# A decoder layer in fp32: an input tile issued earlier, two output tiles moved into the attention, and the last MLP group taken by token tile

## The chip, the cores and the metric

One core of a Trainium2 chip runs the whole layer. The metric is the device time of one execution in microseconds (us). The engines are TensorE (PE, with its weight loads as PEld), VectorE (DVE), ScalarE (ACT), GpSimd (POOL) and SyncE (SP), which here issues every DMA. Each engine runs its own list of instructions in a fixed order and waits on semaphores of the others.

## The reference

```python
c_act = jax.nn.silu(c)
mod = c_act @ w_mod[l] + b_mod[l]                     # 2048 x 12288
sh1, sc1, g1, sh2, sc2, g2 = split(mod, 6)
h = rmsnorm(x, attn_norm_g) * (1.0 + sc1) + sh1       # x: 256 x 2048
proj = h @ w_in                                       # 2048 x 1856
o_a = swa_sink_attention(q_a, k_a, v_a, sinks, rel_bias)   # 16 heads of 64, window 128
c_q, c_kv = rmsnorm(cq part), rmsnorm(ckv part)       # ranks 384 and 128
q_b, kv_b = c_q @ w_uq, c_kv @ w_ukv
o_b = mla_attention(...)                              # 8 heads, causal
x = x + g1 * (concat(o_a, o_b) @ w_out)               # 2048 x 2048
h = rmsnorm(x, mlp_norm_g) * (1.0 + sc2) + sh2
x = x + g2 * (relu(h @ w_ff1) ** 2 @ w_ff2)           # 2048 x 8192 x 2048
return rmsnorm(x, final_norm_g)
```

All of it is float32; a sequence has 256 tokens.

## The kernel before

The 256 tokens lie along the free axis, and the 2048 features are 16 tiles of 128 partitions (`kt`). Every weight is read once, in tiles of about 1 MB, through two rings of buffers: `wm` (tag `rawm`, two slots, and four more in stage 1) for w_mod, and `raw` (three slots) for the rest. All DMAs are issued by SP in program order; one that needs a slot holds up those behind it. The program is written in one order; a scheduler then sets the order of the rows on each engine, and that order is fixed at run time.

*Modulation.* The product with w_mod is not on TensorE: VectorE multiplies a 128 x 2048 tile with the broadcast conditioning vector and sums it (L168, `mod_col`), which gives 128 values of one of the six modulation vectors. 96 such tiles are strewn over the program. Part 1 and 0 (for h) come in stage 1, part 2 (g1) in the attention, parts 4 and 3 (for the second h) in the out projection, part 5 (g2) in the MLP; g2 then goes through DRAM (`g_dr`, a scatter of single elements) to be read back as a row.

*Stage 1.* Step kt takes two modulation tiles, forms h (xn on VectorE L256, h on ScalarE L258), and multiplies it with one w_in tile `wi` in 30 matmul records (L269). The program issues the modulation tiles of kt + 1 ahead of the `wi` tile of kt.

*Attention.* Units 0 to 7 are sliding-window heads (scores L407, minima L336 on VectorE, exponentials on ScalarE, a scaling of the rows L357 on ScalarE or VectorE in turn, transposition L377, values L422), units 8 to 11 the latent heads (`scb`, `ssb`, `ptb`, `pob`). Between them stand fillers, the up-projections from cq and ckv (`pvb`, `puqr`, `pukn`, `puqn`), which need the norms `rq` and `rkv` (`rmsn`, whose last step is L323). Each unit leaves its output in `mix`, split in two parts (L387, L388); mix 0 holds the sliding heads, mix 1 the latent ones.

*Out projection.* Matmuls that need full precision run in a faster form on two-part operands. `split` writes the high part of half a weight tile on ScalarE (L192) and the rest on VectorE (L193). Half 0 takes mix 0, half 1 mix 1; each has 16 output tiles of 24 matmuls (L198 to L200) and an addition to the residual `x_sb` on VectorE (L656). Then the second norm (`r_a`, `r_y`: L180 to L183, with Ln and Exp on ScalarE) lets the MLP's h begin (xn L678 or on GpSimd L680 and L681, h L682 on ScalarE and its second part L683 on VectorE).

*MLP.* ff1's first quarter runs over kt (`pf`), the rest by output tile (`pu`, L204 and L205), ff2 in four q by four column groups c (`pd`, L785 to L787), each group with two PSUM banks, one for each tile t of 128 tokens. In the last group (q = 3, c = 3) VectorE multiplies by g2 (L799), adds the residual (L800) and multiplies by the final gain (L802); ScalarE sums the squares (L801). Then a chain of small operations gives the final norm for each t (L835 to L841), VectorE scales one half of the row (L843), ScalarE the other (L845), and SP sends each off (L844, L846).

Of the kernel before, what the change touches and what calls it, by code (L numbers as in the profile page):

```python
# [54 lines left out]
def kernel(  # L55
# [547 lines left out]


    sqa = keep.tile([P, S], F32, name="sqa")

    class SumSq:

        def __init__(self, name):
            self.name = name

        def add(self, d):
            sq = tmp.tile([P, S], F32, tag="sq", name=f"sq{self.name}{d}", bufs=3)
            A.activation(out=sqa if d == 0 else sq, in_=x_sb[:, d, :], func=AF.Square)
            if 0 < d < 14:
                G.tensor_tensor(out=sqa, in0=sqa, in1=sq, op=ALU.add)
            if d == 14:
                self.pt = bank(f"p{self.name}")  # L620
                T.matmul(self.pt[:, 0:S], lhsT=ones, rhs=sqa, start=True, stop=False)
            if d >= 14:
                T.matmul(self.pt[:, 0:S], lhsT=ones, rhs=sq, start=False, stop=d == 15)

        def rstd(self):
            return rstd(self.pt[:, 0:S], D, self.name, keep)

    ss2 = SumSq("r2")
# [135 lines left out]

    def ff2(q):
# [3 lines left out]
        for c in range(4):  # L769
# [4 lines left out]
            for fg in range(4):  # L774
                w = raw(f"wf2_{q}_{c}_{fg}")
                nc.sync.dma_start(w, w_ff2[q, c, fg])
                for half in range(2):
                    wh, wl = split(w, half, f"wf2_{q}_{c}_{fg}")
                    for t in range(2):
                        for i in range(2):  # L780
                            f = 4 * fg + 2 * half + i
                            u = uu[f // 8][:, f % 8, :]
                            uh, ul = u[:, t * P : (t + 1) * P], u[:, S + t * P : S + (t + 1) * P]
                            o = i * 512
                            T.matmul(pd[t], lhsT=uh, rhs=wh[:, o : o + 512], start=(f == 0), stop=False)  # L785
                            T.matmul(pd[t], lhsT=uh, rhs=wl[:, o : o + 512], start=False, stop=False)  # L786
                            T.matmul(pd[t], lhsT=ul, rhs=wh[:, o : o + 512], start=False, stop=(f == KT - 1))  # L787
# [43 lines left out]


    for t in range(2):
        a, y, z = small(f"f_a{t}"), small(f"f_y{t}"), small(f"f_z{t}")
        V.scalar_tensor_tensor(out=a, in0=ssum[:, 6 + t : 7 + t], scalar=1.0 / D, in1=sbase[:, t : t + 1],  # L835
                               op0=ALU.mult, op1=ALU.add)
        A.activation(out=y, in_=a, func=AF.Ln)
        A.activation(out=y, in_=y, func=AF.Exp, scale=-0.5)
# [101 lines left out]
```

## Time and profile before

| | us |
|---|---|
| median of 3 runs | 1071.34 (1070.76 to 1072.33) |
| the profiled execution | 1074.42 |
| its span, first to last instruction | 1072.4 |
| TensorE busy | 1014.8 (95%) |
| VectorE busy | 723.3 (67%) |
| ScalarE busy | 489.8 (46%) |

Durations come from the profiled execution, whose own time stands 3 us above the median of the runs. The mean granted clock of TensorE is 0.98 of its higher level (2.4 GHz); the rest is spent in stretches at 0.5 (1.2 GHz).

### The profile page before, as it was taken

Reading aid. Unit: us, or ns where it says so; the run is one execution under the profiler, and the core shown is the slowest. Engines: PE = TensorE matmul, PEld = TensorE weight load, DVE = VectorE, ACT = ScalarE, POOL = GpSimd, SP = SyncE. Lnnn points to the kernel's source line nnn. Section 1 sums busy time; section 2 is a strip of 40 time slices with the busy share of each in tenths; the row PEclk is TensorE's granted clock in tenths of the full one; section 3 lists DMA queues with packets and bytes.
Section 4 is the critical chain, followed back from the end, with each engine's and each line's share of the span. In section 5 each row is a group of like instructions: output and inputs, shape, how many; then the busy total and the mean of one; then the engine's idle time right before and its main releaser. Section 6 shows DMA issues by size and latency. Waiting matters only on the chain.

```text
span 1072.4 us, 14192 instructions
## 1 busy us (share of the span) xinstructions
PE 1014.8 (95%) x5582; PEld 869.6 (81%) x5582; DVE 723.3 (67%) x923; ACT 489.8 (46%) x824; POOL 97.1 (9%) x78
## 2 busy tenths in 40 slices
PE   5999988989996999999999999999999999999995
PEld 4777756789995999888887888888888888888884
DVE  5767558889996798797774555455555566555664
ACT  2100077743443443884444656333556533455442
POOL 0000003200255524000000000000000000000120
PEclk9899999989998999999999999999999999999998
DMA  8999976779996776689886655555555555555551
GB/s 327 421 421 420 404 303 220 290 290 372 420 388 258 282 273 259 250 338 345 306 330 216 217 181 177 197 192 196 196 185 174 193 194 196 197 191 180 191 183 79
DMA packets 44259, 280.24 MB, mean 261 GB/s; under 512 B 6880, under 2 KB 9120, under 8 KB 13088
## 3 DMA queue, kind: packets, MB, share of 16 engines
q1 hardware_dynamic: 44192, 279.34, 70.0%
q8 instruction: 43, 0.70, 0.2%
q14 instruction: 24, 0.20, 0.0%
HBM read 277.19 MB, written 2.13 MB: 260 GB/s over the span
## 4 chain that ended last, share of the span: by engine, by line
PE 77%; DMA 8%; DVE 7%; ACT 3%; POOL 2%; issue 2%; SPq 0%; ACTq 0%; DVEq 0%; POOLq 0%
PE pu L204 16%; PE pd L786 10%; PE pd L787 10%; PE pd L785 10%; PE pu L205 8%; PE pj L269 8%; DVE wm L168 3%; DMA wi<-in_w_in 3%; DMA wm<-in_w_mod 3%; PE pd L200 2%; PE pd L199 2%; PE pd L198 2%; PE pf L200 2%; PE pf L198 2%; PE pf L199 2%
## 5 line engine op out<-in xcount | busy, mean ns | idle before, releaser
L193 DVE TENSOR_TENSOR wf_l<-wf,wf_h 128x1024 fp32r<-128x1024 f32 x256 | 317.0, 1240 | 250.6 <-ACT wf_h L192 250.1
L192 ACT ACTIVATE wf_h<-wf 128x1024 fp32r<-128x1024 f32 x256 | 269.9, 1057 | 257.9 <-PE pd L787 183.9
L204 PE MATMUL pu<-h,wf_h 128*128 128x512 f32 x768 | 273.2, 400 | 1.1 <-ACT wf_h L192 1.1
L205 PE MATMUL pu<-h,wf_l 128*128 128x256 f32 x768 | 216.6, 282 | 0.8 <-DVE wf_l L193 0.8
L785 PE MATMUL pd<-wf_h,u 128*128 128x512 f32 x512 | 199.2, 389 | 0.0
L786 PE MATMUL pd<-wf_l,u 128*128 128x512 f32 x512 | 199.2, 389 | 0.0
L787 PE MATMUL pd<-wf_h,u 128*128 128x512 f32 x512 | 199.2, 389 | 0.0
L204 PEld LDWEIGHTS pu<-h,wf_h 128*128 128x128 f32 x768 | 145.0, 189 | 37.4 <-ACT wf_h L192 1.4
L168 DVE CUSTOM_DVE_ANT_0 wm<-wm,c_bc,vec 128x2048 f32<-128x2048 f32 x64 | 153.4, 2399 | 3.8 <-DMA wm<-in_w_mod 3.8
L205 PEld LDWEIGHTS pu<-h,wf_l 128*128 128x128 f32 x768 | 145.9, 190 | 1.5 <-DVE wf_l L193 1.4
L269 PE MATMUL pj<-h,wi 128*128 128x256 f32 (+1 forms) x480 | 112.2, 390 | 12.4 <-ACT h L258 9.9
L269 PEld LDWEIGHTS pj<-h,wi 128*128 128x128 f32 (+1 forms) x480 | 88.6, 190 | 35.9 <-issue 13.8
L785 PEld LDWEIGHTS pd<-wf_h,u 128*128 128x128 f32 x512 | 96.1, 188 | 20.1
L786 PEld LDWEIGHTS pd<-wf_l,u 128*128 128x128 f32 x512 | 96.1, 188 | 19.9
L787 PEld LDWEIGHTS pd<-wf_h,u 128*128 128x128 f32 x512 | 96.1, 188 | 19.9
L168 DVE CUSTOM_DVE_ANT_0 wm<-wm,c_bc,b 128x2048 f32<-128x2048 f32 x32 | 75.8, 2369 | 31.1 <-DMA wm<-in_w_mod 31.1
L198 PE MATMUL pf<-h,wf_h 128*128 128x256 f32 x256 | 73.0, 293 | 7.6 <-ACT h L682 6.1
L200 PE MATMUL pf<-h,wf_l 128*128 128x256 f32 x256 | 72.3, 289 | 4.3 <-DVE wf_l L193 4.3
L200 PE MATMUL pd<-mix,wo_l 128*128 128x256 f32 x256 | 72.8, 285 | 1.4 <-DVE wo_l L193 1.2
L198 PE MATMUL pd<-mix,wo_h 128*128 128x256 f32 x256 | 73.4, 287 | 0.0
L199 PE MATMUL pf<-h,wf_h 128*128 128x256 f32 x256 | 73.1, 288 | 0.1
L199 PE MATMUL pd<-mix,wo_h 128*128 128x256 f32 x256 | 72.4, 283 | 0.0
(187 smaller groups left out, 1039.9 us busy)
## 6 DMA issues: line engine op xcount, KB each, us to landing
wm<-in_w_mod SPq DMA_DIRECT2D x96, 1024.0 KB, 8.0
wf<-in_w_ff SPq DMA_DIRECT2D x64, 1024.0 KB, 4.8
wf<-in_w_ff1b SPq DMA_DIRECT2D x48, 1024.0 KB, 4.9
wo<-in_w_out SPq DMA_DIRECT2D x16, 1024.0 KB, 11.0
wf<-in_w_ff1a SPq DMA_DIRECT2D x16, 1024.0 KB, 7.2
wi<-in_w_in SPq DMA_DIRECT2D x15, 928.0 KB, 12.5
x_sb<-in_xT SPq DMA_DIRECT2D x4, 512.0 KB, 5.6
bias<-g_dr SPq DMA_DIRECT2D x2, 1024.0 KB, 14.1
```

The costliest lines, as they stand in the source:

```text
L168: V.tensor_tensor_reduce(out=t, in0=t, in1=c_bc, scale=1.0, scalar=init, op0=ALU.mult, op1=ALU.add, accum_out=col)
L192: A.activation(out=hi, in_=src, func=AF.Copy)
L193: V.tensor_tensor(out=lo, in0=src, in1=hi.bitcast(F32), op=ALU.subtract)
L198: T.matmul(out, lhsT=wh, rhs=a[:, 0:S], start=start, stop=False, **kw)
L199: T.matmul(out, lhsT=wh, rhs=a[:, S : 2 * S], start=False, stop=False, **kw)
L200: T.matmul(out, lhsT=wl, rhs=a[:, 0:S], start=False, stop=stop, **kw)
L204: T.matmul(out, lhsT=wh, rhs=a, start=start, stop=False)
L205: T.matmul(out[:, 0:S], lhsT=wl, rhs=a[:, 0:S], start=False, stop=stop)
L269: T.matmul(proj(j)[: e - j * P, :], lhsT=w[:, j * P : e], rhs=h, start=(kt == 0 and j % 2 == 0), stop=(kt == KT - 1), skip_group_check=True)
L785: T.matmul(pd[t], lhsT=uh, rhs=wh[:, o : o + 512], start=(f == 0), stop=False)
L786: T.matmul(pd[t], lhsT=uh, rhs=wl[:, o : o + 512], start=False, stop=False)
L787: T.matmul(pd[t], lhsT=ul, rhs=wh[:, o : o + 512], start=False, stop=(f == KT - 1))
```

## The change

It has three parts. In stage 1, `stage1_w(kt)` issues the w_in tile of kt ahead of the modulation tiles of kt + 1. In the attention, the two norms `rmsn` are called between the scores and the minima of the first pair of units, and the first two output tiles of half 0 (`out_tile(0, 0)` and `out_tile(0, 1)`, both from the first weight tile `wo_0`) are called ahead of the turns of units 10 and 11. In the last group of ff2, all products of token tile 0 come first; the split weights are kept (six in space of `a0`, `a1` and `u`, two in the split ring), then come the products of token tile 1, and `final(t)` is called for each t at once. No instruction is added on any engine. What the program's new order makes of the rows elsewhere is the scheduler's doing.

```diff
     def split(w, half, name, into=None):
+        hi, lo = into or [splp.tile([P, 1024], F32R, tag=f"w{i}", name=f"{name}_{i}{half}") for i in ("hi", "lo")]
...
-    def stage1_mm(kt, h):
-        w = raw(f"wi{kt}")
+    def stage1_w(kt):
+        w = raw(f"wi{kt}")
...
+        return w
+
+    def stage1_mm(kt, w, h):
...
     for kt in range(KT):
+        w = stage1_w(kt)
         if kt + 1 < KT:
             hs[kt + 1] = stage1_mod(kt + 1)
-        stage1_mm(kt, hs.pop(kt))
+        stage1_mm(kt, w, hs.pop(kt))
...
-    def swa_scores(u0, u1):
+    def swa_scores(u0, u1, *between):
...
-        u0.minima()
-        u1.minima()
+        for u, f in zip((u0, u1), between or (None, None)):
+            if f:
+                f()
+            u.minima()
...
+    def out_tile(half, d):
+        dp, d2 = divmod(d, 2)
+        if d2 == 0:
+            wo[half] = raw(f"wo{half}_{dp}")
+            nc.sync.dma_start(wo[half], w_out[half, dp])
+        wh, wl = split(wo[half], d2, f"wo{half}_{dp}")
+        pd = bank(f"pd{half}_{d}")
+        for k in range(8):
+            o = k * P
+            mm3(pd[:, 0:S], wh[:, o : o + P], wl[:, o : o + P], mix[half][:, k, :], k == 0, k == 7)
+        V.scalar_tensor_tensor(out=x_sb[:, d, :], in0=pd[:, 0:S], scalar=g1[d], in1=x_sb[:, d, :],
+                               op0=ALU.mult, op1=ALU.add)
...
-        swa_scores(units[0], units[1])
+        swa_scores(units[0], units[1], lambda: rmsn(cq, V_GQ, 384, "rq"), lambda: rmsn([ckv], V_GKV, 128, "rkv"))
         va_turn()
-        rmsn(cq, V_GQ, 384, "rq")
-        rmsn([ckv], V_GKV, 128, "rkv")
...
+            if n >= 10:
+                out_tile(0, n - 10)
             u.turn()
...
             for d2 in range(2):
                 d = 2 * dp + d2
...
+                if half or dp:
+                    out_tile(half, d)
...
+            last = q == 3 and c == 3
+            kept = []
...
+            if last:
+
+                homes = [actp.tile([P, 4, 1024], F32R, tag=f"a{i}", name=f"kept{i}") for i in range(2)]
+                homes.append(up_pool.tile([P, 4, 1024], F32R, tag="u", name="kept2"))
+                homes = [(h[:, 2 * i, :], h[:, 2 * i + 1, :]) for h in homes for i in range(2)]
+            for g in range(8):
...
+                wh, wl = split(w, g % 2, f"wf2_{q}_{c}_{g // 2}", homes[g] if last and g < 6 else None)
+                products(0, g, wh, wl)
+                if last:
+                    kept.append((wh, wl))
+                else:
+                    products(1, g, wh, wl)
...
+            for t in range(2):
+                if t:
+                    for g, (wh, wl) in enumerate(kept):
+                        products(1, g, wh, wl)
...
+                if last:
+                    final(t)
```

On SP, from the end of the program's start on, the tiles came in this order before (`wm_1` is a pair of modulation tiles of step 1, `wi` the w_in tile, step 0's first):

```order
10 L233 DMA g_dr<-g_sb 16x384
11 L161 DMA wm_1_207<-in_w_mod 128x2048 x2
12 L266 DMA wi_220<-in_w_in 128x1856
13 L161 DMA wm_2_237<-in_w_mod 128x2048 x2
14 L266 DMA wi_250<-in_w_in 128x1856
15 L161 DMA wm_3_267<-in_w_mod 128x2048
16 L161 DMA wm_3_271<-in_w_mod 128x2048
17 L266 DMA wi_281<-in_w_in 128x1856
```

and after:

```order
10 L232 DMA g_dr<-g_sb 16x384
11 L265 DMA wi_207<-in_w_in 128x1856
12 L161 DMA wm_1_209<-in_w_mod 128x2048 x2
13 L265 DMA wi_237<-in_w_in 128x1856
14 L161 DMA wm_2_239<-in_w_mod 128x2048 x2
15 L265 DMA wi_267<-in_w_in 128x1856
16 L161 DMA wm_3_269<-in_w_mod 128x2048
17 L161 DMA wm_3_273<-in_w_mod 128x2048
```

Each `wi` now stands one pair further ahead.

On TensorE, at the attention's end, the last two units' value products (`pob`) and transpositions (`ptb`) and the first products of half 0 (`pd_0`) stood thus before:

```order
306 L481 MATMUL pob_1416<-pTb_1388,vB 128x128
307 L377 MATMUL ptb_1427<-ident,ssb_1353 128x128 x4
308 L481 MATMUL pob_1444<-pTb_1432,vB 128x128 x4
309 L377 MATMUL ptb_1451<-ident,ssb_1400 128x128 x4
310 L377 MATMUL ptb_1458<-ident,ssb_1400 128x128 x4
311 L481 MATMUL pob_1465<-pTb_1456,vB 128x128
312 L198 MATMUL pd_0_1483<-mix_684,wo_0_h_1479 128x256
313 L199 MATMUL pd_0_1483<-mix_684,wo_0_h_1479 128x256
314 L200 MATMUL pd_0_1483<-mix_684,wo_0_l_1480 128x256
```

and after, where the 24 products of `pd_0` and of `pd_1` stand whole:

```order
302 L486 MATMUL pob_1417<-pTb_1389,vB 128x128
303 L197 MATMUL pd_0_1434<-mix_684,wo_0_hi_1430 128x256
304 L198 MATMUL pd_0_1434<-mix_684,wo_0_hi_1430 128x256
305 L199 MATMUL pd_0_1434<-mix_684,wo_0_lo_1431 128x256
...
326 L199 MATMUL pd_0_1434<-mix_684,wo_0_lo_1431 128x256
327 L380 MATMUL ptb_1460<-ident,ssb_1354 128x128 x4
328 L486 MATMUL pob_1477<-pTb_1465,vB 128x128 x4
329 L197 MATMUL pd_1_1488<-mix_684,wo_0_hi_1484 128x256
330 L198 MATMUL pd_1_1488<-mix_684,wo_0_hi_1484 128x256
```

All of the first output tile stands ahead of unit 10's transposition, and the second (rows 329 to 352) ahead of unit 11's. On VectorE the same place, from the split of `wo_0`'s second half to the scaling of unit 10's rows (`ssb_1353`), read before:

```order
262 L193 TENSOR_TENSOR wo_0_l_1510<-wo_0_1477,wo_0_h_1509 128x1024
263 L388 TENSOR_TENSOR mix_1335<-pob_1369,mix_1335 128x4x128
264 L193 TENSOR_TENSOR wo_1_l_1542<-wo_1_1539,wo_1_h_1541 128x1024
265 L168 ISA wm_12_740,mod_12_742<-wm_12_740,c_bc,vec 128x2048
266 L168 ISA mod_12_742 128x1
267 L336 ISA ssb_1400,mb_1401<-scb_1390,con 128x256
...
275 L348 RECIPROCAL smb_1406<-smb_1406 128x4
276 L388 TENSOR_TENSOR mix_1335<-pob_1416,mix_1335 128x4x128
277 L357 TENSOR_SCALAR ssb_1353<-ssb_1353,smb_1406 128x128 x4
278 L348 RECIPROCAL smb_1434<-smb_1434 128x4
279 L168 ISA wm_13_744,mod_13_746<-wm_13_744,c_bc,vec 128x2048
```

and after (the unit's rows are `ssb_1354`):

```order
260 L391 TENSOR_TENSOR mix_1336<-pob_1370,mix_1336 128x4x128
261 L192 TENSOR_TENSOR wo_0_lo_1485<-wo_0_1428,wo_0_hi_1484 128x1024
262 L351 RECIPROCAL smb_1407<-smb_1407 128x4
263 L360 TENSOR_SCALAR ssb_1354<-ssb_1354,smb_1407 128x128
264 L339 ISA ssb_1401,mb_1402<-scb_1391,con 128x256
...
272 L360 TENSOR_SCALAR ssb_1354<-ssb_1354,smb_1407 128x128 x3
273 L168 ISA wm_11_736,mod_11_738<-wm_11_736,c_bc,vec 128x2048
...
275 L391 TENSOR_TENSOR mix_1336<-pob_1417,mix_1336 128x4x128
276 L168 ISA wm_12_740,mod_12_742<-wm_12_740,c_bc,vec 128x2048
...
278 L536 SCALAR_TENSOR_TENSOR x_sb<-pd_0_1434,mod_0_694,x_sb 128x256
279 L192 TENSOR_TENSOR wo_1_lo_1542<-wo_1_1539,wo_1_hi_1541 128x1024
```

The mod tile (wm_12 before, wm_11 after) now stands behind unit 11's scores and unit 10's scalings.

On VectorE, at the second norm, the rows before were:

```order
386 L168 ISA wm_7_2758,mod_7_2760<-wm_7_2758,c_bc,vec 128x2048
...
391 L182 TENSOR_TENSOR r_a<-r_a,r_y 128x256
392 L193 TENSOR_TENSOR wf_l_2661<-wf_2624,wf_h_2660 128x1024
393 L183 SCALAR_TENSOR_TENSOR r_y<-r_a,r_y 128x256
394 L193 TENSOR_TENSOR wf_l_2702<-wf_2688,wf_h_2701 128x1024
395 L678 SCALAR_TENSOR_TENSOR xn_0_2632<-x_sb,a_0_2630,r_y 128x256
396 L168 ISA wm_8_2827,mod_8_2829<-wm_8_2827,c_bc,b_124 128x2048
...
405 L168 ISA wm_8_2896,mod_8_2898<-wm_8_2896,c_bc,vec 128x2048
...
407 L193 TENSOR_TENSOR wf_l_2730<-wf_2688,wf_h_2729 128x1024
```

and after:

```order
390 L182 TENSOR_TENSOR r_a<-r_a,r_y 128x256
391 L183 SCALAR_TENSOR_TENSOR r_y<-r_a,r_y 128x256
392 L192 TENSOR_TENSOR wf_lo_2661<-wf_2624,wf_hi_2660 128x1024
393 L691 SCALAR_TENSOR_TENSOR xn_0_2632<-x_sb,a_0_2630,r_y 128x256
394 L192 TENSOR_TENSOR wf_lo_2702<-wf_2688,wf_hi_2701 128x1024
...
397 L168 ISA wm_7_2758,mod_7_2760<-wm_7_2758,c_bc,vec 128x2048
...
401 L168 ISA wm_8_2827,mod_8_2829<-wm_8_2827,c_bc,b_124 128x2048
...
403 L192 TENSOR_TENSOR wf_lo_2730<-wf_2688,wf_hi_2729 128x1024
...
409 L168 ISA wm_8_2896,mod_8_2898<-wm_8_2896,c_bc,vec 128x2048
```

r_y now stands ahead of the split, and the split of the third half tile (`wf_l_2730` before, `wf_lo_2730` after) ahead of the second wm_8 tile.

## Rows read from the trace of the kernel before

**Rows 1.** The page, TensorE's line: busy us, share of the span, instructions.

```profile
PE 1014.8 (95%) x5582; PEld 869.6 (81%) x5582; DVE 723.3 (67%) x923; ACT 489.8 (46%) x824; POOL 97.1 (9%) x78
```

**Rows 2.** Windows (stretch, length, busy of PE, PEld, DVE, ACT, POOL; PEclk, DMA share, GB/s).

```profile
30.00:90.00 60.00, 60.00 (x258) 47.90 (x257) 43.29 (x52) 4.80 (x8) 0.00 (x0) 0.97 1.01 421
...
140.00:227.00 87.00, 74.22 (x411) 54.13 (x410) 71.86 (x183) 62.35 (x195) 15.97 (x14) 0.94 0.69 257
227.00:275.00 48.00, 46.57 (x384) 45.96 (x383) 43.66 (x51) 16.60 (x17) 0.00 (x0) 1.00 0.93 369
```

**Rows 3.** TensorE's waits, whole run: waited for, us in total, times, longest.

```profile
PE pf L198 <- ACT h L682: 6.1, 1, 6.1
PE pf L200 <- DVE wf_l L193: 4.3, 4, 3.0
...
PE ptb L377 <- DVE ssb L357: 3.6, 1, 3.6
PE pvb L536 <- DVE ckv L323: 2.9, 1, 2.9
...
PE pu L204 <- ACT wf_h L192: 1.1, 1, 1.1
```

**Rows 4.** The chain of waits (start, us, what), stage 1's end and 564.

```profile
114.21 15.03 DMA wi<-in_w_in
...
129.37 10.51 PE pj L269 x46
...
563.98 16.24 DMA wf<-in_w_ff1b
```

**Rows 5.** Timeline of stage 1's end: start, us, engine, instruction, idle before it.

```profile
129.15 0.60 ACT L258 ACTIVATE h<-xn,mod,a 128x256 f32<-128x256 f32 x1 [6.67 <-DVE mod L168]
```

**Rows 6.** SP's waits from 20 to 125: in total, times, longest.

```profile
SPq L266 <- PE pj L269: 73.9, 13, 9.1
```

**Rows 7.** The page's DMA issues: count, KB each, median us to landing.

```profile
wi<-in_w_in SPq DMA_DIRECT2D x15, 928.0 KB, 12.5
```

**Rows 8.** VectorE's timeline in the attention.

```profile
154.73 0.47 DVE L323 SCALAR_TENSOR_TENSOR ckv<-ckv,vec,rkv_y 128x256 f32<-128x256 f32 x1
...
213.57 2.35 DVE L168 CUSTOM_DVE_ANT_0 wm<-wm,c_bc,vec 128x2048 f32<-128x2048 f32 x1 [0.93 <-DMA wm<-in_w_mod]
```

**Rows 9.** TensorE's timeline near the attention's end.

```profile
218.37 1.12 PE L377 MATMUL ptb<-ident,ssb 128*128 128x128 f32 x4 [3.56 <-DVE ssb L357]
```

**Rows 10.** Windows around the stretches at the lower clock (columns as in rows 2).

```profile
213.00:229.00 16.00, 11.75 (x76) 10.94 (x76) 12.33 (x24) 7.15 (x18) 0.00 (x0) 0.79 0.67 229
347.00:352.00 5.00, 4.48 (x25) 4.48 (x26) 1.95 (x3) 2.40 (x3) 1.91 (x2) 0.66 0.91 316
583.00:587.00 4.00, 4.00 (x16) 3.43 (x15) 2.00 (x3) 3.42 (x6) 0.00 (x0) 0.57 1.02 428
```

**Rows 11.** VectorE's timeline after the second norm's sum.

```profile
329.03 1.22 DVE L193 TENSOR_TENSOR wf_l<-wf,wf_h 128x1024 fp32r<-128x1024 f32 x1
...
343.43 2.89 DVE L168 CUSTOM_DVE_ANT_0 wm<-wm,c_bc,vec 128x2048 f32<-128x2048 f32 x1
```

**Rows 12.** Timeline of the end, all engines.

```profile
1058.95 0.70 DVE L799 TENSOR_TENSOR pd<-pd,g_row 128x512 f32<-128x512 f32 x1 [4.48 <-PE pd L787]
...
1059.66 0.39 PE L786 MATMUL pd<-wf_l,u 128*128 128x512 f32 x1
...
1059.88 0.39 PE L787 MATMUL pd<-wf_h,u 128*128 128x512 f32 x1
1060.31 0.70 DVE L799 TENSOR_TENSOR pd<-pd,g_row 128x512 f32<-128x512 f32 x1
...
1063.97 2.19 ACT L845 ACTIVATE xt<-xt,f_y 128x1024 f32<-128x1024 f32 x2 [0.36 <-DVE f_y L841]
...
1066.47 1.18 SPq L846 DMA_DIRECT2D out_tok<-xt  x1
```

**Rows 13.** The output's DMAs, issue to landing.

```profile
DMA to landing us min/median/max: 2.6/4.0/4.9
```

More of the change, by code (lines that the diff above doesn't have):

```diff
@@ L185, in rstd, with split @@
         return y
-    def split(w, half, name):
-        hi = splp.tile([P, 1024], F32R, tag="whi", name=f"{name}_h{half}")
-        lo = splp.tile([P, 1024], F32R, tag="wlo", name=f"{name}_l{half}")
+    def split(w, half, name, into=None):
+        hi, lo = into or [splp.tile([P, 1024], F32R, tag=f"w{i}", name=f"{name}_{i}{half}") for i in ("hi", "lo")]
         src = w[:, half * 1024 : (half + 1) * 1024]
@@ L491, in rope, with __init__, add, rstd @@
         G.tensor_tensor(out=t, in0=t, in1=u, op=ALU.add)
+    sqa = keep.tile([P, S], F32, name="sqa")
+    class SumSq:
+        def __init__(self, name):
+            self.name = name
+        def add(self, d):
+            sq = tmp.tile([P, S], F32, tag="sq", name=f"sq{self.name}{d}", bufs=3)
+            A.activation(out=sqa if d == 0 else sq, in_=x_sb[:, d, :], func=AF.Square)
+            if 0 < d < 14:
+                G.tensor_tensor(out=sqa, in0=sqa, in1=sq, op=ALU.add)
+            if d == 14:
+                self.pt = bank(f"p{self.name}")
+                T.matmul(self.pt[:, 0:S], lhsT=ones, rhs=sqa, start=True, stop=False)
+            if d >= 14:
+                T.matmul(self.pt[:, 0:S], lhsT=ones, rhs=sq, start=False, stop=d == 15)
+        def rstd(self):
+            return rstd(self.pt[:, 0:S], D, self.name, keep)
+    ss2 = SumSq("r2")
+    wo = {}
+    def out_tile(half, d):
[10 more added lines that the diff above has]
+                               op0=ALU.mult, op1=ALU.add)
     with tc.high_priority():
@@ L602 @@
                 swa_values(units[n - 1], u)
[L605 to L628, printed above, removed]
     def to_tokens(dp):
@@ L773, in ff2, with products @@
             cs = slice(c * 512, (c + 1) * 512)
[L774 to L787, printed above, removed]
+            last = q == 3 and c == 3
+            kept = []
+            def products(t, g, wh, wl):
+                for i in range(2):
+                    f = 2 * g + i
+                    u = uu[f // 8][:, f % 8, :]
+                    uh, ul = u[:, t * P : (t + 1) * P], u[:, S + t * P : S + (t + 1) * P]
+                    o = i * 512
+                    T.matmul(pd[t], lhsT=uh, rhs=wh[:, o : o + 512], start=(f == 0), stop=False)
+                    T.matmul(pd[t], lhsT=uh, rhs=wl[:, o : o + 512], start=False, stop=False)
+                    T.matmul(pd[t], lhsT=ul, rhs=wh[:, o : o + 512], start=False, stop=(f == KT - 1))
+            if last:
[3 more added lines that the diff above has]
+            for g in range(8):
+                if g % 2 == 0:
+                    w = raw(f"wf2_{q}_{c}_{g // 2}")
+                    nc.sync.dma_start(w, w_ff2[q, c, g // 2])
+                wh, wl = split(w, g % 2, f"wf2_{q}_{c}_{g // 2}", homes[g] if last and g < 6 else None)
[4 more added lines that the diff above has]
+                    products(1, g, wh, wl)
             if q == 2 and c == 1:
@@ L830 @@
     ff2(3)
[L833 to L838, printed above, removed]
-        V.scalar_tensor_tensor(out=z, in0=a, scalar=-0.5, in1=y, op0=ALU.mult, op1=ALU.mult)
-        V.tensor_tensor(out=z, in0=z, in1=y, op=ALU.mult)
-        V.scalar_tensor_tensor(out=y, in0=z, scalar=1.5, in1=y, op0=ALU.add, op1=ALU.mult)
-        lo, hi = xt[:, t, 0:1024], xt[:, t, 1024:2048]
-        V.tensor_scalar(out=lo, in0=lo, scalar1=y, scalar2=None, op0=ALU.mult)
-        nc.sync.dma_start(out[t, :, 0:1024], lo)
-        A.activation(out=hi, in_=hi, func=AF.Copy, scale=y)
-        nc.sync.dma_start(out[t, :, 1024:2048], hi)
 def _constants():
```

23 lines of the change are left out of this document (14 added, 9 removed).

## The prediction

> **What bounds the kernel now.** I read the page's summary first, then a table of windows by stage, then TensorE's waits, and last the single rows around the places that the diff touches. The page says that TensorE is busy for 95% of the span [rows 1], so the most that any reordering can win is TensorE's idle time, some 58 us, and the stretches at the lower of its two clocks. The windows say where that lies [rows 2]. From 30 to 90 us the DMA queues are full at 421 GB/s while TensorE is busy throughout; from 140 to 227 (attention) TensorE lacks 12.8 us and VectorE 15.1; from 227 to 275 (out projection, half 0) TensorE lacks 1.4 and VectorE 4.3. So the attention has room, but only as much as VectorE's static order leaves. The list of waits names the pieces [rows 3]; those at the start of the program aside, five of them bear on the change.
>
> **Part one, `wi` ahead of the next `wm` pair.** It adds and removes no instruction; it swaps 0.95 MB with 2.1 MB on SP's queue, sixteen times. At the end of the stage TensorE waits for w_in's tiles: the tile of step 14 is issued at 114.21 and lands 15.03 later, at 129.24; 46 matmuls from 129.37 on take 10.51, so the thirty of a step 6.85, and step 15 begins at 136.2 [rows 4]. h of step 15 is ready long before that: ScalarE writes it from 129.15 to 129.75, as soon as VectorE has summed the last mod tile [rows 5]. The order of landing is thus wm_15 twice, wi_14, wi_15. After the change it is wi_14, wm_15 twice, wi_15. At 421 GB/s a w_in tile is 2.26 us and a mod tile 2.49. wi_14 lands two mod tiles earlier, at 124.3; h of step 15 comes one w_in tile later, at 129.75 + 2.26 = 132.0. Step 14 then starts one period earlier than 15 (2.26 + 2 x 2.49 = 7.24), at 124.8, and is done by 131.7. Step 15 begins at 132.0 in place of 136.2: -4.2. TensorE's first matmul comes some 5 us earlier too, but that only lets it wait for each h later on. I take **-4.0**, with 0 (nothing comes of it) and -4.2 as ends. The clock costs nothing here, as TensorE stays 6.85 of 7.24 busy.
>
> The DMA stream itself cannot end sooner, as it runs at 421 GB/s and no byte is saved [rows 2]. In the Trainium skill, DMA: Bandwidth & Descriptors, "Where 436 GB/s comes from" puts a fixed ceiling of about 435 GB/s on a core's ports, whatever the order of issue. Here 421 GB/s agrees with it. Taken alone, that rule makes this part worth 0, and the sum below 4 less; the rows on 129.24 and 129.75 say that the last wait is for one tile out of order, not for the last byte.
>
> What SP's new order queues behind a wait: SP waits before w_in's tile for a slot, 13 times on TensorE and 9.1 us at the longest [rows 6], and now wm_(k+1) stands behind that wait, where before it had been issued. From the end of step k-3, which frees the slot, three steps (3 x 7.24 = 21.7) lie until h_(k+1) is needed. Issue to landing of w_in's tile is 12.5 [rows 7], two mod tiles more are 5.0, the sum of one and h are 2.35 + 0.6 [rows 5, 8]: 20.5. It fits by 1.2.
>
> **Part two, attention and out projection.** (i) The norms of cq and ckv move ahead of minima. Now VectorE writes ckv only at 154.73, its chain of four operations threaded between the second pair's minima; TensorE waits 2.9 for it [rows 3, 8]. In the new order the chain stands ahead of the second pair's minima, so those minima leave it, and it starts before them. The wait should go, and what is late next are the second pair's minima; they lie under the up-projections that ckv sets free. (ii) The first two output tiles move inside. TensorE stalls 3.56 before 218.37 for a VectorE scaling that stands behind the mod tile of 213.57, which had itself waited 0.93 for its DMA [rows 3, 8, 9]. In the new order a tile of 24 matmuls (46.57/16 = 2.9 us [rows 2]) stands just ahead of that transposition, and one of the four scalings and the next scores have moved ahead of the mod tile. Of this some 3.5 should go. (iii) The stall drops TensorE to its low level: the granted clock is 0.79 from 213 to 229 [rows 10], so 0.21 x 11.75 busy us = 2.5 us are lost, and a busy TensorE keeps them. No work is added: the splits (1.24 on VectorE) are those of before, earlier. Sum: 2.9 + 3.5 + 2.5 = 8.9. I take **-9.0**.
>
> Its bounds: all of TensorE's idle time from 140 to 275 (14.2) plus 2.5 is -16.7, which VectorE's 19.5 idle us there would just let through [rows 2]; the other end is 0, where VectorE's chain moves as a whole and TensorE finds the waits elsewhere. I stay nearer the middle because in half 0 TensorE's waits are already small and VectorE is 91% busy.
>
> **Part two's echo at the second norm.** The scheduler moves VectorE's rows there as well. A split of 1.22, at 329.03, stands between L182 and r_y, and after the change it stands behind r_y: about -1.1 off the wait of 6.1 for h. A second split stands behind a mod tile of 2.89 begun at 343.43, and TensorE waits 3.0 for it, then runs at 0.66 of the clock from 347 to 352 (0.34 x 4.48 = 1.5 lost) [rows 3, 10, 11]. After, this split stands ahead of the mod tile. All of it is -5.6; nothing is the other end, since two mod tiles (2.35 each [rows 8]) now stand among h1 to h4, which TensorE needs every 48 matmuls. I take **-3.5**.
>
> **Modulation at 580.** A scatter of g2 through DRAM stands on SP's queue, and a weight tile issued behind it, at 563.98, lands only 16.24 later [rows 4]; TensorE waits 1.1 for its first half's split [rows 3], and then for the second's. In the new order wm_15 is one SP row and one VectorE split earlier, so the scatter goes out up to a mod tile's time, 2.35 and some, earlier. From 0 to -2.0, and -1.7 more if the low clock of 583 to 587 (0.57) [rows 10] goes with it; I take **-1.0**.
>
> **Part three, the last group.** TensorE's last product ends when it did, after the same 96 matmuls. Before, both token tiles end together: VectorE's L799 begins for t0 at 1058.95 and for t1 at 1060.31, and the two epilogues share VectorE and ScalarE, so that ScalarE's two scalings end at 1063.97 + 2.19 = 1066.16, the fourth output DMA goes out at 1066.47, and it lands up to 4.9 later, at 1071.4 [rows 12, 13]. After, t0's epilogue lies under t1's 48 products (some 10.6 us, as one starts 0.22 after the other). t0's way from L799 to its scaling now takes 1063.97 - 1058.95 = 5.0, with two VectorE operations of t1 (0.70 each) in it; for t1 alone 3.6 remain, so its scaling runs from 1063.9 to 1065.0 and the DMA goes out at 1065.3. It lands after 2.6 (the first of four now) to 4.0 (their median) [rows 13], 3.3 in the middle: 1068.6. **-2.7**, with -2.0 and -3.5 as ends. That six splits are kept longer costs nothing on the engines: they go to space that the earlier stages left, and VectorE's 4.48 idle us before 1058.95 [rows 12] show that it has room.
>
> **Sum.** -4.0 - 9.0 - 3.5 - 1.0 - 2.7 = -20.2. The profiled execution took 1074.42 for a span of 1072.4; 1074.42 - 20.2 = 1054.2, and scaled to the median of the runs (1071.34/1074.42) 1051.2. I predict **1051 us**.
>
> **Rivals.** *VectorE binds* (0.15). The mod tiles with their two slots and the splits form one chain from 200 to 275; if its length is what counts, part two gives 1 at most and its echo 1: 4 + 1 + 1 + 3 = 9, **1062 us**. For it: VectorE is 91% busy in half 0, and mod tiles still wait for their DMA there. Against it: VectorE still idles 15.1 in the attention.
> *All of it comes* (0.10): 4.2 + 13 + 5.6 + 2.5 + 3.2 = 28.5, **1043 us**. For it: each of the waits is named and its releaser moves up. Against it: where a wait goes, a smaller one behind it shows.
> *The bytes decide* (0.08): the swap in stage one does nothing, everything else holds: 1071.3 - 16.2 = **1055 us**.
> *Starved mod tiles* (0.05), the one on the other side: if 20.5 becomes more than 21.7, each us over it lengthens three steps by 1, so fifteen steps by 5. 3.2 us over cost 16 and cancel what the other parts bring (16.2), which is the point from which it decides; five cost 25 and end at 1071.3 + 25 - 16.2 = **1080 us**. For it: SP's 73.9 us of waiting in this place [rows 6]. Against it: a queue that is less full also lands sooner.
>
> **Chances.** The forecast has 0.62. The measurement tells about 0.2% (2 us). Faster: 0.62 + 0.15 + 0.10 + 0.08 = 0.95; of the starved case 0.03 is slower and 0.02 within 0.2%. The range runs from the full gain to VectorE's case, 1043 to 1063; the forecast's own is 1046 to 1057, from the middle halves of the terms' bounds.
>
> **What would show it.** In the profile after: step 15 of L269 begins near 132 and waits for ScalarE's h, no longer for the DMA; no wait of TensorE above 1.5 us between 140 and the out projection, and no low clock after 213 of before's time; half 0 ends some 13 us earlier; the wait for h at the second norm is about 5, and the 3.0 behind it is gone; VectorE's L799 for t0 comes some 11 us before that for t1, and the last output lands about 8.5 us after TensorE's last product. I am wrong if stage one's steps grow beyond 7.3 us, or if VectorE's mod tiles end at the same time as now.

## The result and the profile after

| | us |
|---|---|
| before, median of 4 runs | 1071.05 (1069.03 to 1072.33) |
| after, median of 4 runs | 1052.81 (1050.44 to 1053.02) |
| ratio | 0.9826, 95% interval 0.9805 to 0.9847 |
| the profiled execution after, its span | 1053.02, 1051.2 |

The changed kernel is 18.2 us faster; the forecast was 20 (1051). In a later measurement beside other kernels the ratio was 0.9829 (0.9803 to 0.9855).

**Stage 1.** The chain of waits at the stage's end (start, us, what), which answers to [rows 4]:

```profile
110.41 15.97 DMA wm<-in_w_mod
...
126.40 2.35 DVE wm L168
...
128.95 2.32 DVE wm L168
...
131.38 0.61 ACT h L257
```

It now runs over the mod tiles, no longer over `wi`: a mod tile lands at 126.38, VectorE sums the pair, ScalarE writes h. TensorE's timeline of the last two steps:

```profile
124.76 6.89 PE L271 MATMUL pj<-h,wi 128*128 128x256 f32 x30 [0.35 <-ACT h L257]
132.03 3.72 PE L271 MATMUL pj<-h,wi 128*128 128x256 f32 x16 [0.39 <-ACT h L257]
```

Step 15 begins at 132.03, where 132.0 was forecast, and what it waited for is h. The exact hit is partly luck: in a second profile of the same kernel the whole DMA stream came 2.3 us sooner and step 15 began at 129.76. A step lasts 7.27, so no mod tile starves.

**Attention.** Windows after (columns as in [rows 2]): the attention, half 0, and three stretches to compare with [rows 10].

```profile
136.00:222.00 86.00, 79.93 (x498) 61.48 (x495) 76.98 (x189) 64.46 (x198) 14.38 (x14) 1.00 0.77 288
222.00:264.00 42.00, 40.70 (x332) 39.80 (x332) 39.62 (x49) 14.46 (x15) 0.00 (x0) 1.00 0.97 385
203.00:220.00 17.00, 14.98 (x122) 14.16 (x121) 16.10 (x26) 9.41 (x21) 0.00 (x0) 1.00 0.78 278
339.00:344.00 5.00, 5.00 (x32) 5.00 (x31) 4.25 (x5) 2.52 (x3) 1.65 (x2) 0.66 0.90 375
410.00:415.00 5.00, 4.02 (x21) 4.02 (x22) 4.47 (x4) 0.00 (x0) 4.92 (x2) 0.66 0.00 0
```

In the attention TensorE now lacks 6.1 us where it lacked 12.8, at full clock throughout; VectorE's share has risen from 83% to 90%. Half 0 ends at 259.5 in place of 274.6, which is 15.1 us earlier; some 13 were forecast. TensorE's timeline at its end, against [rows 9]:

```profile
203.81 0.36 PE L197 MATMUL pd<-mix,wo_hi 128*128 128x256 f32 x1
...
206.78 0.60 PE L380 MATMUL ptb<-ident,ssb 128*128 128x128 f32 x4
208.45 1.16 PE L486 MATMUL pob<-pTb,vB 128*128 128x128 f32 x8 [1.07 <-ACT pTb L370]
```

The first output tile runs from 203.8 to 206.8, and unit 10's transposition follows it without a wait. What is left are waits for ScalarE's copies, 1.1 and 0.9. TensorE's waits of the whole run, against [rows 3]:

```profile
PE pj L271 <- ACT h L257: 7.8, 11, 4.0
PE pf L199 <- DVE wf_lo L192: 5.9, 5, 2.3
PE pf L197 <- ACT h L695: 5.0, 1, 5.0
...
PE prq L492 <- ACT qr L370: 3.2, 4, 1.3
PE pob L486 <- ACT pTb L370: 2.0, 2, 1.1
```

`ptb` and `pvb` are gone; the wait for h at the second norm is 5.0 (from 6.1). But `pf` waits 5.9 in all for VectorE's splits, where it waited 4.3: in place of the one wait of 3.0, which the forecast had going, stand three of 0.7, 0.8 and 1.8, and the windows show the low clock near 340 and again near 412. The second norm's stage has not become shorter.

**The end.** All engines' timeline:

```profile
1031.01 0.70 DVE L845 TENSOR_TENSOR pd<-pd,g_row 128x512 f32<-128x512 f32 x1 [2.66 <-PE pd L814]
...
1041.46 0.39 PE L814 MATMUL pd<-wf_hi,u 128*128 128x512 f32 x1
1041.89 0.70 DVE L845 TENSOR_TENSOR pd<-pd,g_row 128x512 f32<-128x512 f32 x1 [6.59 <-PE pd L814]
...
1045.41 1.15 ACT L791 ACTIVATE xt<-xt,f_y 128x1024 f32<-128x1024 f32 x1 [0.67 <-DVE f_y L787]
...
1046.58 0.43 SPq L792 DMA_DIRECT2D out_tok<-xt  x1
```

and the output's DMAs from issue to landing:

```profile
DMA to landing us min/median/max: 2.7/3.2/3.7
```

VectorE's first row for t0 stands 10.9 us ahead of that for t1. From the end of TensorE's last product (1041.85) to the end of the span it is 9.4; before it was 12.1, by [rows 12] and the span.

### The profile page after: what moved, and what is told of

It reads as the page before. It is cut to its first block, busy times and chain, and to the rows that moved or that the text cites. A ratio compares the mean times of both kernels' runs of the same rounds, so it can differ in the third digit from the quotient of the medians.

```text
span 1051.2 us, 14181 instructions
## 1 busy us (share of the span) xinstructions
PE 1008.8 (96%) x5582; PEld 866.6 (82%) x5582; DVE 723.2 (69%) x923; ACT 487.4 (46%) x824; POOL 101.2 (10%) x78
## 4 chain that ended last, share of the span: by engine, by line
PE 73%; DVE 10%; DMA 8%; ACT 4%; POOL 2%; issue 2%; SPq 0%; ACTq 0%; DVEq 0%; POOLq 0%
PE pu L203 17%; PE pd L814 11%; PE pd L812 11%; PE pd L813 11%; PE pu L204 9%; DMA wm<-in_w_mod 7%; DVE wm L168 5%; PE pj L271 5%; PE pf L199 2%; PE pf L198 2%; PE pf L197 2%; POOL xn L693 1%; DVE wo_lo L192 1%; DMA wo<-in_w_out 1%; ACT ssa L349 1%
## 5 line engine op out<-in xcount | busy, mean ns | idle before, releaser
L192 DVE TENSOR_TENSOR wf_lo<-wf,wf_hi 128x1024 fp32r<-128x1024 f32 x250 | 308.5, 1239 | 222.9 <-ACT wf_hi L191 222.3
L191 ACT ACTIVATE wf_hi<-wf 128x1024 fp32r<-128x1024 f32 x250 | 263.7, 1056 | 238.0 <-PE pd L814 169.1
L203 PE MATMUL pu<-h,wf_hi 128*128 128x512 f32 x768 | 270.2, 397 | 0.0
L204 PE MATMUL pu<-h,wf_lo 128*128 128x256 f32 x768 | 215.5, 281 | 0.0
L812 PE MATMUL pd<-wf_hi,u 128*128 128x512 f32 x488 | 189.9, 389 | 0.0
L814 PE MATMUL pd<-wf_hi,u 128*128 128x512 f32 x488 | 189.9, 389 | 0.0
L813 PE MATMUL pd<-wf_lo,u 128*128 128x512 f32 x488 | 189.9, 389 | 0.0
L204 PEld LDWEIGHTS pu<-h,wf_lo 128*128 128x128 f32 x768 | 145.1, 189 | 0.1
L814 PEld LDWEIGHTS pd<-wf_hi,u 128*128 128x128 f32 x488 | 91.6, 188 | 19.0
L812 PEld LDWEIGHTS pd<-wf_hi,u 128*128 128x128 f32 x488 | 91.6, 188 | 19.0
L197 PE MATMUL pf<-h,wf_hi 128*128 128x256 f32 x256 | 74.0, 293 | 6.1 <-ACT h L695 5.0
L197 PE MATMUL pd<-mix,wo_hi 128*128 128x256 f32 x256 | 73.9, 289 | 1.3 <-ACT wo_hi L191 1.3
L198 PE MATMUL pf<-h,wf_hi 128*128 128x256 f32 x256 | 74.4, 292 | 0.0
L198 PE MATMUL pd<-mix,wo_hi 128*128 128x256 f32 x256 | 72.5, 283 | 0.0
## 6 DMA issues: line engine op xcount, KB each, us to landing
wo<-in_w_out SPq DMA_DIRECT2D x16, 1024.0 KB, 12.1
```

The costliest lines, as they stand in the source:

```text
L197: T.matmul(out, lhsT=wh, rhs=a[:, 0:S], start=start, stop=False, **kw)
L198: T.matmul(out, lhsT=wh, rhs=a[:, S : 2 * S], start=False, stop=False, **kw)
L203: T.matmul(out, lhsT=wh, rhs=a, start=start, stop=False)
L204: T.matmul(out[:, 0:S], lhsT=wl, rhs=a[:, 0:S], start=False, stop=stop)
```

## Where the time went, and what varies by itself

One profile of each kernel doesn't settle this: the difference of the two spans is 21.2 us, that of the medians 18.2. So every run was cut at the same marks, each a start or an end of one record in its timeline: the landing of w_in's last piece, the first matmul of step 15 (L269 before), the end of half 1, ff1(2)'s first product (where ff1's first quarter, the `pf` stage, has ended), ff1(3)'s, ff2(1)'s, and the last product. Differences of these marks, in us:

| | landing to step 15 | step 15 to half 1's end | from there to ff1(2) | ff1(3) to ff2(1) | last product to end |
|---|---|---|---|---|---|
| before | 4.54 | 188.8 | 111.4 | 94.3 | 12.1 |
| before again | 4.58 | 186.6 | 111.4 | 90.8 | 12.2 |
| part three alone | 4.57 | 191.1 | 111.4 | 91.1 | 9.4 |
| part one alone | 0.77 | 187.6 | 111.4 | 91.7 | 12.1 |
| norms alone | 4.58 | 183.2 | 111.4 | 91.1 | 12.1 |
| part two alone | 4.58 | 178.7 | 112.3 | 93.7 | 12.2 |
| part one and tiles | 0.77 | 182.6 | 116.0 | 90.4 | 12.2 |
| changed | 0.78 | 178.2 | 113.2 | 89.1 | 9.4 |
| changed again | 0.79 | 179.1 | 113.3 | 90.4 | 9.5 |

The columns move with the parts, apart from the second and the fourth, which have a spread of their own in the kernel before: 186.6 to 191.1 and 90.8 to 94.3 in the three profiles with its rows there. In the changed kernel's 89.1 the products of that stretch follow each other a little faster than in its second profile (90.4); its rows show no cause for that.

## The experiments

**The kernel before again.** All three parts undone in the changed kernel's code; on each engine its rows stand in the order of the kernel before.

> The kernel before once more, written with the changed kernel's helpers and all three parts undone, so that its second profile shows what varies by itself. Theory (the change won 5 us near 580 by moving the last g2 tile on SP): TensorE's two waits there (1.1 and 0.8) and the low clock after them come again, ratio 1.000. Rival (that stretch was an accident of one profiled execution, whose 1074.4 stands 3 above the median): no such waits in this profile, its span near 1069, ratio 1.000.

Measured: 1069.05 us, ratio 0.9977 (0.9962 to 0.9992), and a profile with a span of 1063.4. Two programs with the same rows thus came out 0.23% apart, with an interval that leaves out 1; differences of that size say nothing here, and where this one comes from stays open. The profile is 9.0 us shorter than the first: 3.2 until step 15 (w_in's last piece landed at 128.35 in place of 131.62), 2.2 in the attention, 3.6 near 580. There the wait came again, smaller:

```profile
PE pu L204 <- DVE wf_lo L192: 0.8, 1, 0.8
```

and without the low clock. Neither theory was right as put: the wait belongs to the kernel, its size and the low clock to the execution.

**Part one alone.**

```diff
     for kt in range(KT):
+        w = stage1_w(kt)
         if kt + 1 < KT:
             hs[kt + 1] = stage1_mod(kt + 1)
-        w = stage1_w(kt)
```

> Only the w_in tile is issued ahead. Theory (the last wait is for one tile out of order): the last step of stage 1 begins at 132.0 in place of 136.2, and since SP's and VectorE's rows behind the attention stay as before, the 4 us last to half 1's end (320.8 in place of 325.0); some 1 to 2 may be given back in ff1's first quarter, where VectorE's mod tiles pace TensorE. Ratio 0.9965 (0.996 to 0.998). Rival (the bytes decide): step 15 at 136, ratio 1.000. Second rival (mod tiles starve): steps over 7.3 us, ratio above 1.005.

Measured: 1065.54, ratio 0.993 (0.9908 to 0.9951). Step 15 begins at 132.30. Set against the first profile that is the 4 us that were expected, but before-again's begins at 132.93, right behind a step 14 that waited for its `wi`:

```profile
126.14 10.51 PE L271 MATMUL pj<-h,wi 128*128 128x256 f32 x46 [0.40 <-DMA wi<-in_w_in]
```

What the part changes is the distance to the landing of w_in's last piece: 4.54 to 4.58 without it, 0.77 to 0.79 with it, 3.8 us, whenever the stream ends. Neither rival held: the bytes ended where they would, and the last eight steps stayed at 7.23 to 7.30. Nothing of it was given back in ff1's first quarter (111.4). The timed gain is larger than 3.8 us (its interval begins at 5.2) and than the range that was expected; before-again's 2 us show how much can lie between two programs without a cause in their rows, and against before-again's 1069.05 the gain is 3.5.

**Part two alone.**

```diff
-        swa_scores(units[0], units[1])
+        swa_scores(units[0], units[1], lambda: rmsn(cq, V_GQ, 384, "rq"), lambda: rmsn([ckv], V_GKV, 128, "rkv"))
         va_turn()
-        rmsn(cq, V_GQ, 384, "rq")
-        rmsn([ckv], V_GKV, 128, "rkv")
...
+            if n >= 10:
+                out_tile(0, n - 10)
             u.turn()
...
```

> Only the norms and the two output tiles are moved. Theory (the attention's waits are won by themselves): TensorE's waits for ckv (2.9) and for unit 10's scaling (3.6) are gone and no stretch at the low clock lies between 200 and 300; half 1 ends at 314 to 315 in place of 325.0. At the second norm a split now stands ahead of each of the last steps of the norm, so the wait for h is longer by 1 to 2, and g2's place on SP is that of before, so the waits near 580 stay. Ratio 0.992 (0.990 to 0.994). Rival (VectorE's chain binds, and the gain needs stage 1 to end sooner): half 1 ends at 321 or later, ratio above 0.996.

Measured: 1063.14, ratio 0.9921 (0.9902 to 0.9941). Both waits and the low clock are gone, half 1 ends at 313.6, and step 15 to half 1's end is 178.7, as in the changed kernel. The gain doesn't need part one. Of the 1 to 2 us expected at the second norm 0.5 came, 0.9 by the end of that stage, and the waits near 580 stayed (1.3 and 0.8).

**Part three alone.** (`last = q == 3 and c == 3`, the rest as before.)

> Only the last group of ff2 goes by token tile. Theory: nothing before the last group moves; from TensorE's last product to the end 9.3 us in place of 12.1, which is 2.8 less, ratio 0.9974 (0.996 to 0.999). Rival (the output's transfer is the floor): the end stays 12 after the last product, ratio 1.000.

Measured: 1068.36, ratio 0.9974 (0.9958 to 0.999). Last product to end is 9.4, the theory's 2.8 less. The timed ratio fits, but lies as near to that of before-again, so the profile, not the time, is what shows it.

**The norms alone, and part one with the tiles.** Two kernels that split part two.

> Only the norms of cq and ckv are moved. Theory (each piece of part two wins its own wait): TensorE's wait of 2.9 for ckv is gone, the wait before unit 10's transposition (2.5 to 3.6) and the low clock after it stay; from step 15 to half 1's end 184 to 186, where the old order has 186.6 to 191.1 and part two whole 178.7. Rival (the norms bring nothing without the tiles): 188 or more.

> Part one with the two output tiles, without the norms' move and the last group's. It is the smallest combination in which SP's order near 580 becomes that of the changed kernel (the last g2 tile one place ahead), and VectorE's order at the second norm nearly so. Theory (that order, not chance, wins the waits near 580): no wait of TensorE there, and from the second to the third output quarter of ff1 44.7 us, where the runs with the old order have 46.4 to 49.1. Rival (chance): 46.4 or more, with waits of 0.8 or more. Theory on ff1's first quarter (VectorE begins it one mod tile behind): 113.2 from half 1's end to the quarter's end, as in the changed kernel, where the old order has 111.4; rival (the loss comes from the norms' move): 111.4.

Measured: 1063.3 and 1064.3 in one run each, beside 1068.61 for the kernel before. Of the norms alone, TensorE's wait and the window at the attention's end:

```profile
PE ptb L380 <- DVE ssb L360: 2.9, 1, 2.9
```

```profile
200.00:222.00 22.00, 18.41 (x126) 16.50 (x125) 18.36 (x38) 13.32 (x36) 0.00 (x0) 0.84 0.76 277
```

With the tiles and without the norms, the other wait and the same window:

```profile
PE pvb L582 <- DVE ckv L326: 2.9, 1, 2.9
```

```profile
200.00:225.00 25.00, 23.29 (x183) 20.75 (x182) 24.96 (x47) 17.88 (x44) 0.00 (x0) 1.00 0.90 344
```

Each piece wins its own wait: the norms remove `pvb` and leave `ptb` with the clock at 0.84, the tiles remove `ptb` and keep the clock at 1.00 but leave `pvb`. From step 15 to half 1's end they bring some 5 each (188 to 183, where 184 to 186 was expected, and 187.6 to 182.6), and together 10. Each is one profile against an old order that by itself lies between 186.6 and 191.1, so how the 10 divide is known only to within some 2 us.

The second kernel also has the changed kernel's order on SP near 580, and there its TensorE doesn't wait, as in the other profiles with that order (the changed kernel twice, and with xn on VectorE, below). All six profiles with the old order have the wait, 0.2 to 2.1 us in all. SP's timeline in the changed kernel and in before-again:

```profile
548.08 0.38 SPq L832 DMA_DIRECT2D g_dr<-g_all  x1
550.36 1.03 SPq L757 DMA_DIRECT2D wf<-in_w_ff1b  x1
```

```profile
557.34 0.38 SPq L831 DMA_DIRECT2D g_dr<-g_all  x1
558.48 0.33 SPq L756 DMA_DIRECT2D wf<-in_w_ff1b  x1
```

The scatter goes out 7.6 us ahead of ff1(3)'s first product (555.68) in the one, 6.1 ahead of it (563.41) in the other; with part one and the tiles it is 8.8. The tile behind it lands 7.9 after that product in the changed kernel and no later in the other profiles without the wait, 9.4 to 11.3 after it in the six; the wait begins somewhere between. From ff1(3)'s first product to ff1(4)'s it takes 45.2 us with part one and the tiles, 0.5 above the theory and below all six (45.8 to 49.1).

In ff1's first quarter the run with part one and the tiles lost more than the changed kernel, 116.0 against the old 111.4; so the loss comes with the order that the tiles bring together with part one, not with the norms' move. Neither expectation had its size; its VectorE rows there are not quite those of the changed kernel, and its last mod tile begins 103.4 us behind half 1's end in place of 101.8.

**Without the last mod tiles; xn on VectorE.** Two kernels on that loss. In the first, steps 14 and 15 have no modulation tiles of their own and take the scale and shift of step 13; in the second their xn is computed on VectorE.

```diff
-    modq = [(p, i) for i in range(KT) for p in (4, 3)]
+    modq = [(p, i) for i in range(KT - 2) for p in (4, 3)]
...
+        for m in (sc2, sh2):
+            m.setdefault(kt, m.get(KT - 3))
...
```

```diff
-        if kt < 1:
+        if kt < 1 or kt >= 14:
             V.scalar_tensor_tensor(out=xn, in0=x_sb[:, kt, :], scalar=a2, in1=r2, op0=ALU.mult, op1=ALU.mult)
```

> The changed kernel without the last four modulation tiles of parts 4 and 3 (steps 14 and 15 take the scale and shift of step 13), so 9.4 us less on VectorE and 4 MB less to load at the end of ff1's first quarter. Theory (VectorE's mod tiles pace the end of that quarter): the 4.0 us between the last steps go away, half 1's end to the quarter's end is 109 in place of 113.2. Rival (GpSimd's xn, 5.1 us a step, paces it): the steps 14 and 15 still come late, 112 or more. The g2 scatter goes out earlier still, so no wait near 580 either.

> The changed kernel with xn of steps 14 and 15 on VectorE (0.9 us each) in place of GpSimd (5.1 each). Rival theory (GpSimd's xn paces the end of ff1's first quarter): 4 us less, 109 to 110 from half 1's end to the quarter's end. Theory (VectorE's mod tiles pace it, the shift's tile is needed anyway): at most 1 us less, 112 to 114.

Measured, one run each: 1049.87 and 1052.04. From half 1's end to ff1(2) it is 108.1 without the tiles, and 112.0 with xn on VectorE, against 113.2. TensorE's waits from 384 to 424 in the first:

```profile
PE pf L199 <- DVE wf_lo L192: 0.8, 1, 0.8
PE pf L197 <- ACT wf_hi L191: 0.8, 1, 0.8
```

and in the second:

```profile
PE pf L199 <- DVE wf_lo L192: 3.6, 2, 2.8
PE pf L197 <- ACT wf_hi L191: 0.2, 1, 0.2
```

Taking four mod tiles from VectorE takes 5.1 us from the stage; taking 5 us a step from GpSimd's chain takes 1.2. VectorE's work sets the end of that stage, GpSimd only adds to it. The 4 MB that the first kernel doesn't load are not the reason: in the changed kernel no computing engine waits for a DMA between 310 and 424. The first kernel's scatter goes out 22.8 us ahead of ff1(3), and near 580 nothing waits.

**The mod tiles further ahead.** If VectorE's idle time early in that stage could take a tile, the loss should shrink.

```diff
-LEADK = (1, 1)
+LEADK = (2, 1)
```

Three kernels: this one, the same with xn of steps 14 and 15 on VectorE, and (2, 2). The changed kernel ran beside them.

> The changed kernel with the modulation tiles of ff1's first quarter pumped two ahead at even steps (LEADK = (2, 1)), so that VectorE takes wm_8 where it idles between h1 and h4, and so that g2's scatter comes out during ff2's first group. Theory (VectorE's mod tiles pace the end of that quarter, and idle time at its start is the reserve): from half 1's end to the quarter's end 110 to 111 in place of 113.2 (112.0 in the other profile), no wait near 580; ratio to before 0.980 (0.978 to 0.982). Rival (the slots or the DMA set when the mod tiles come): 113 or more, ratio 0.983.

> The run with the mod tiles two ahead, and xn of steps 14 and 15 on VectorE as well. Theory: the 1.2 us that this gave to the changed kernel come on top, 109 to 110, ratio 0.979. Rival (once VectorE is ahead, GpSimd's xn is hidden): no difference from the other, within 0.3.

> The changed kernel with the tiles pumped two ahead at every step (LEADK = (2, 2)); here a mod tile and two splits stand ahead of the norm's last step. Theory: the norm costs 1.5 to 2 more (8.5 to 9 in place of 7.14 from half 1's end to the first product), the end of the quarter 3 to 4 less: 111 to 112 in all, ratio 0.981. Rival (the slots decide): 114 or more.

> The changed kernel once more, on the same chip as these, for a comparison without the spread between executions. Both theories: ratio to before 0.982 to 0.984.

Measured: 1072.05, ratio 1.001 (0.9994 to 1.0025); 1070.57, 1.0 (0.9985 to 1.0015); 1080.38, 1.0086 (1.006 to 1.0112); and the changed kernel 1053.08, 0.9829. The theory failed in all three: half 1's end to ff1(2) became 129.6, 129.1 and 137.7. That lies within the rival's open bounds (113 or more, 114 or more), but not for its reason: in that stage no computing engine waits for a DMA in the first two kernels, and in the third VectorE does once, for 0.4. TensorE's wait in the first:

```profile
PE pf L197 <- ACT wf_hi L191: 14.1, 7, 4.2
```

and ScalarE's, VectorE's and GpSimd's rows at one of the seven:

```profile
370.91 0.51 ACT L695 ACTIVATE h<-xn,mod 128x256 fp32r<-128x256 f32 x1 [6.43 <-POOL xn L694]
371.32 1.99 ACT L191 ACTIVATE wf_hi<-wf 128x1024 fp32r<-128x1024 f32 x2
...
372.40 2.36 DVE L192 TENSOR_TENSOR wf_lo<-wf,wf_hi 128x1024 fp32r<-128x1024 f32 x2 [0.46 <-ACT wf_hi L191]
374.67 2.35 DVE L168 CUSTOM_DVE_ANT_0 wm<-wm,c_bc,b 128x2048 f32<-128x2048 f32 x1
...
377.38 2.89 POOL L693 TENSOR_SCALAR xn<-x_sb,a 128x256 f32<-128x256 f32 x1 [6.51 <-issue]
...
381.12 0.51 ACT L695 ACTIVATE h<-xn,mod 128x256 fp32r<-128x256 f32 x1 [7.80 <-POOL xn L694]
```

The rows form a ring. GpSimd forms xn of a step once VectorE has summed its mod tile; ScalarE writes h from it, and its splits stand behind that h; VectorE's split waits for ScalarE's, and the next mod tile stands behind VectorE's split. One turn takes 10.2 us (370.91 to 381.12), a step of TensorE 5.76. With tiles pumped ahead, h of a later step came to stand ahead of the splits of an earlier one on ScalarE (the last of the 16 h has 24 splits of ff1's tiles ahead of it, in the changed kernel 30), and TensorE waited for the ring seven times. A version that beats the changed kernel beyond doubt was not found.

## Why the prediction was right, and which step of it failed

Its terms against the marks (old against new, means of the profiles in the table whose rows in that stage are those of before and those of the changed kernel):

| term | forecast | measured |
|---|---|---|
| part one | -4.0 | -3.8 |
| part two | -9.0 | -10.2 (188.8 to 178.6) |
| its echo at the second norm | -3.5 | +1.8 (111.4 to 113.2) |
| modulation at 580 | -1.0 | -1.9 (92.1 to 90.2) |
| part three | -2.7 | -2.7 (12.1 to 9.4) |
| sum | -20.2 | -16.8 |

The sum agrees with the timed difference, whose interval is 16.4 to 20.9 us. In the fourth line the means are over six old and five new profiles, the two experiments on the mod tiles among the new. That the time came within 2 us of the forecast is partly luck: the echo was off by 5.3, part two and 580 brought 2.1 more than forecast, and the 1.4 between -16.8 and the timed 18.2 is within what two programs with the same rows differ by.

*Part one* went as worked out: h of step 15 a w_in tile later, `wi` no longer last. The Trainium skill, DMA: Bandwidth & Descriptors, "Where 436 GB/s comes from", taken alone, had spoken against it. Its ceiling holds, with 421 GB/s again from 30 to 90 us, which is more than the 358 or so that the same section lets HBM give one core. The stage's end followed the order of two tiles all the same.

*Part two* was a little larger than forecast, and each of (i) and (ii) with (iii) brought about 5. In (i) I counted the wait for ckv alone, 2.9. In the norms alone the first up-projection (`pvb`) comes 3.2 earlier after step 15 (15.9 in place of 19.1) and the next (`puqr`) 4.4 to 4.9 earlier (20.3 in place of 24.7 to 25.2 in the old order); where the rest of the difference comes from is not shown.

*The echo* is the step that failed, and it failed in sign. Its first piece was right: r_y ahead of the split took 1.08 from half 1's end to the first product (8.22 to 7.14). Its second was wrong in kind. I priced a wait in the middle of ff1's first quarter (3.0) as gained when its split moved ahead of the mod tile, and looked for the price among h1 to h4. The mod tiles didn't vanish: 17 lie between half 1's end and ff1(2) in both kernels. Before, the first of them began 0.4 us behind half 1's end and ended just as VectorE began the norm (L180, at 327.67), so it cost nothing:

```profile
325.41 2.34 DVE L168 CUSTOM_DVE_ANT_0 wm<-wm,c_bc,vec 128x2048 f32<-128x2048 f32 x1
```

In the changed kernel VectorE idles in its place, waiting for ScalarE, and the tile comes behind the norm, 8.4 behind half 1's end:

```profile
312.88 0.42 DVE L180 TENSOR_SCALAR r_a<-pr 128x256 f32<-128x256 f32 x1 [2.08 <-ACT r_y L178]
...
318.61 2.34 DVE L168 CUSTOM_DVE_ANT_0 wm<-wm,c_bc,vec 128x2048 f32<-128x2048 f32 x1
```

Part two alone leaves the tile where it was, and its stage is 112.3; part one with the tiles moves it as the changed kernel does, 116.0. The stage ends where VectorE's tiles end. By its products, 48 a step, TensorE begins step 13 at 90.2 us behind half 1's end in the changed kernel and at 92.4 before, so 2.2 of the 3.5 had been won by then; from there to ff1(2) it takes 23.0 in place of 19.0. The timeline of the last steps in the changed kernel:

```profile
398.37 2.35 DVE L168 CUSTOM_DVE_ANT_0 wm<-wm,c_bc,b 128x2048 f32<-128x2048 f32 x1
...
401.09 2.85 POOL L693 TENSOR_SCALAR xn<-x_sb,a 128x256 f32<-128x256 f32 x1 [3.70 <-DVE a L688]
404.02 2.21 POOL L694 TENSOR_TENSOR xn<-xn,r_y 128x256 f32<-128x256 f32 x1
...
406.26 0.51 ACT L695 ACTIVATE h<-xn,mod 128x256 fp32r<-128x256 f32 x1 [6.43 <-POOL xn L694]
406.68 1.99 ACT L191 ACTIVATE wf_hi<-wf 128x1024 fp32r<-128x1024 f32 x2
...
407.21 2.34 DVE L168 CUSTOM_DVE_ANT_0 wm<-wm,c_bc,b 128x2048 f32<-128x2048 f32 x1
...
409.70 2.36 DVE L192 TENSOR_TENSOR wf_lo<-wf,wf_hi 128x1024 fp32r<-128x1024 f32 x2
...
407.77 0.39 PE L197 MATMUL pf<-h,wf_hi 128*128 128x256 f32 x1 [0.93 <-ACT wf_hi L191]
...
410.98 0.58 PE L199 MATMUL pf<-h,wf_lo 128*128 128x256 f32 x1 [2.35 <-DVE wf_lo L192]
```

From the first mod tile of one step to that of the next (398.37 to 407.21) the ring takes 8.8 us: the tile, GpSimd's xn 5.1, h, its second part. TensorE's step takes 5.76, so in step 14 it waits 0.9 and 2.3, and it drops to the low clock (0.66 from 410 to 415 in the windows above). The experiment without these tiles shows that it is this work; I had named VectorE as the rival bound for the attention, where it was not, and not for this stage, where it was.

*At 580* the direction held; how much it is worth does not come out of these profiles, as -1.0 and -1.9 both lie within what single executions vary.

Of the rivals, *VectorE binds* and *starved mod tiles* did not come, *the bytes decide* is out by the first column, and *all of it comes* (28.5) fell short by 7.4 at the echo and by 2.8 in part two.

## What to carry to other kernels

Where a stream of tiles is at its bandwidth, ask which tile the consumer waits for after the last byte that it needs: the order of two DMAs was worth 3.8 us with not a byte saved. A wait removed in the middle of a stage can be worth nothing if the stage's last rows belong to another engine's fixed amount of work: add up that engine's work over the whole stage first, and see which of it runs now where nobody waits for it. And cut several profiles at common marks before a difference of 2 us is given a cause.
